# Tile addresses at one residue modulo 512 bytes, and the transposed input loaded into another tile, in a two-layer hybrid encoder trunk

## The chip, the cores and the metric

One core of one Trainium2 chip runs the whole program in one launch. The metric is the device time of one execution in microseconds (us); a kernel's time is the median of its runs. An execution that the hardware profiler records has a time of its own, and beside it a span, from the first instruction to the last.

## The reference, cut to what matters

Two layers over 256 tokens of width 2048. In each layer the normalised input `h` is multiplied by one wide matrix, `w_in`, and four branches (a recurrence, a differential attention, a latent attention and an attention into 256 memory tokens) are computed from parts of the product, gated, projected by `w_branch`, merged and projected by `w_out`:

```python
for l in range(DEPTH):                       # 2 layers
    h = _rms_norm(x, norm_g[l])              # x: (1, 256, 2048), float32
    p = h @ w_in[l]                          # (2048, 14784)
    ...
    mem_n = _rms_norm(mem, mem_norm_g[l])    # mem: (1, 256, 2048)
    y_d = _mem_attention(m_q, mem_n, mem_w_kv[l], mem_qk_g[l])
    gates = gate_in.reshape(B, S, N_BRANCH, BRANCH_WIDTH)
    merges = merge_in.reshape(B, S, N_BRANCH, D_MODEL)
    z = None
    for bi, y in enumerate((y_a, y_b, y_c, y_d)):
        zb = jax.nn.sigmoid(merges[:, :, bi]) * (
            (y.astype(x.dtype) * jax.nn.silu(gates[:, :, bi])) @ w_branch[l, bi])
        z = zb if z is None else z + zb
    x = x + z @ w_out[l]
```

All of it is float32. The kernel writes each large product as three products of rounded halves: `hi*hi + hi*lo + lo*hi`.

## The kernel before, in words

**The weight stream.** `jobs` (L491) lists the large products of a layer in the order in which TensorE is to run them: the keys and values of the memory (`mem_w_kv`, two jobs of 512 columns), the recurrence's columns of `w_in` (`e_u`, four jobs), then the other columns of `w_in`, `w_branch` and `w_out`. `main` (L564) walks that list. For every two blocks of 128 weight rows it loads a tile `raww` from HBM by a DMA on SP's queue (L584, three buffers); for each block, `split` (L166) rounds the weights to a tile `whi` on ScalarE (ACT) and puts the rest into `wlo` on VectorE (DVE), five buffers each. `product` (L624) issues three matmuls per block and output bank. In most jobs the activations are the stationary operand, 128 columns at a time (512 bytes in each partition), and `whi` or `wlo` is streamed, 512 columns wide (2,048 bytes). In the jobs with `tpos` set (the recurrence's columns and the gates) it is the other way round: slices of `whi` and `wlo` are stationary and the activations are streamed, 256 columns wide.

**The activations.** `mT`, the transposed memory, lies in the tiles S0 to S7. `hT`, the normalised input transposed, lies in T1h (the rounded half) and T1l (the rest), 16 blocks each. The gated branch results lie in ygh and ygl. The merged branches, `z`, are transposed by `z_prep` (L797) for the `w_out` jobs, two blocks at a time, into eight different places: X, iA, BK with qr, q1, T1h, k1, T1l, V1.

**Where tiles lie.** The pool `work` gives each tag its place in the order in which the tags are first asked for, in steps of 32 bytes. In the built program the starts of the tiles, in bytes modulo 512 (the residue), are:

| tiles | residue before | residue after |
|---|---|---|
| raww, whi, wlo, q1, Z | 448 | 128 |
| T1h, T1l, V1, raw | 416 | 128 |
| PT, X, S0 to S7, U, ygh | 320 | 128 |
| E, jk | 480 | 128 |
| iA, BK, qr, k1, ygl, sg, yT, r1 to r3 | 224 | 128 |

Every slice that a matmul takes of these tiles as an operand of 512 bytes or more starts a multiple of 512 bytes into its tile, so the residue of the tile is the residue of the operand.

**The start of the program.** `mem_prep(0)` (L349) loads the transposed memory into U and ygh by eight DMAs on ACT's queue and splits it into S0 to S7, while the two `mem_w_kv` jobs run. `x_first` (L406) then prepares `hT` of the first layer. It loads the transposed input (`xT`, four DMAs of 512 KB, L414) into the same places, three quarters into U and one into ygh, once the memory's blocks there are used up. Squares on ACT (L420), sums on DVE (L423 to L427), a matmul with ones (L430), a power on POOL (L433), a copy, two transposes on TensorE (L438) and a copy (L440) give the tile r4, the inverse norms spread over the partitions. Then eight chunks of two blocks are multiplied by gain and norm on DVE (L449) and split: ACT writes T1h, DVE writes T1l (L451). The event `("hT", 0)` (L454) is set after the eighth chunk, and the first `w_in` job waits for it (L525). Afterwards `token_sums` (L386) loads the memory once more, not transposed, into Z, for the norms of the memory.

**What sets the order.** The Python program runs generators (lanes) beside `main`; a scheduler then orders the instructions of each engine by a simulated timeline. `high_priority` lifts instructions in that order, and `issue_after` keeps one behind another. The weights' loads, splits and evacuations run with the priority HP. `self.last` holds the last split's two instructions, so that `issue_after(self.last[1])` puts an instruction behind the newest `wlo`. A job may have a `kready`, an event that each of its 128-row blocks waits for; before, the first memory job and the `w_out` jobs have one.

Of the kernel before, what the change touches and what calls it, by code (L numbers as in the profile page):

```python
# [29 lines left out]
C_ID, C_MF, C_MB, C_BLK, C_CEN, C_B2, C_MH, C_IF, C_OH, C_N = (  # L30
    0, 128, 256, 384, 512, 640, 642, 658, 690, 694)
# [14 lines left out]
XE = 5.0  # L46
# [7 lines left out]
def _constants():  # L54
    c = np.zeros((128, C_N), np.float32)
    c[:, C_ID:C_ID + 128] = np.eye(128)
    s = np.arange(128)[:, None] % 64
    t = np.arange(64)[None, :]
    c[:, C_MF:C_MF + 64] = s < t
    c[:, C_MF + 64:C_MF + 128] = s <= t  # L60
    c[:, C_MB:C_MB + 64] = s > t
    c[:, C_MB + 64:C_MB + 128] = s >= t
    blk = (np.arange(128)[:, None] // 64 == np.arange(128)[None, :] // 64).astype(np.float32)
    c[:, C_BLK:C_BLK + 128] = blk
    c[:, C_CEN:C_CEN + 128] = np.eye(128) - blk / 64
    c[:, C_B2:C_B2 + 2] = blk[:, [0, 64]]
    c[:, C_MH:C_MH + 16] = -0.5
# [45 lines left out]
class Builder:  # L113
# [65 lines left out]
        self.nc.gpsimd.tensor_tensor(ss, ss, self.cst[:, C_MH:C_MH + n], op=ALU.pow)  # L179

    def small(self, n):
        return self.t("small", [128, 16], bufs=6)[:, :n]


    def setup(self):
        nc, a = self.nc, self.a
# [162 lines left out]
    def mem_prep(self, l):  # L349

        nc, a = self.nc, self.a
        T = [self.t(f"S{i}", [128, 4, 256], F32R) for i in range(8)]
        X3 = self.t("U", [128, 3, 4, 256])
# [18 lines left out]
        for i in range(8):  # L372
            if not l and 1 <= i <= 4:
                with self.tc.issue_after(self.last[0]):
                    load(i + 3)
            if not l and i == 3:
                with self.tc.issue_after(self.fetch):
                    nc.sync.dma_start(self.cst, a["consts"])
            for kk in (2 * i, 2 * i + 1):
                j, k = kk // 4, kk % 4  # L380
                with self.tc.high_priority(2 * HP if kk < (4 if l else 2) else 0):
                    self.split(T[j][:, k], T[4 + j][:, k], X[j][:, k], scale=g[:, kk:kk + 1])
                self.ev.add(("mT", l, kk))
            yield 0.0

    def token_sums(self, src, rs):  # L386
# [16 lines left out]
        self.rsqrt(rs, 2, 1.0 / D, EPS)  # L403
        yield

    def x_first(self):  # L406

        nc, a = self.nc, self.a
        yield from self.until(("mT", 0, 15))
        X3 = self.t("U", [128, 3, 4, 256])  # L410
        X = [X3[:, j] for j in range(3)] + [self.t("ygh", [128, 4, 256])]
        for j in range(4):
            with self.tc.issue_after(self.last[0]):
                nc.scalar.dma_start(X[j], a["xT"][:, 4 * j:4 * j + 4])  # L414

        sq = self.t("T1l", [128, 4, 1024])
        yield XE
        for j in range(4):
            with self.tc.issue_after(self.last[0]):
                nc.scalar.activation(sq[:, j], X[j].rearrange("p k t -> p (k t)"), AF.Square)  # L420
            if j % 2:
                with self.tc.issue_after(self.last[1]):
                    nc.vector.tensor_tensor(sq[:, j - 1], sq[:, j - 1], sq[:, j], op=ALU.add)  # L423
            yield
        nc.vector.tensor_tensor(sq[:, 0], sq[:, 0], sq[:, 2], op=ALU.add)
        nc.vector.tensor_tensor(sq[:, 0, 0:512], sq[:, 0, 0:512], sq[:, 0, 512:1024], op=ALU.add)
        nc.vector.tensor_tensor(sq[:, 0, 0:256], sq[:, 0, 0:256], sq[:, 0, 256:512], op=ALU.add)  # L427
        ps = self.pa()
        for tt in range(2):
            self.mm(ps[:, 2 * tt:2 * tt + 2], sq[:, 0, tt * 128:tt * 128 + 128], self.ones)  # L430
        rs = self.small(2)
        nc.vector.tensor_scalar(rs, ps[:, 0:4:2], 1.0 / D, EPS, op0=ALU.mult, op1=ALU.add)
        nc.gpsimd.tensor_tensor(rs, rs, self.cst[:, C_MH:C_MH + 2], op=ALU.pow)  # L433
        ex = self.t("sq", [128, 2, 128])
        nc.vector.tensor_copy(ex, rs[:, :, None].to_broadcast([128, 2, 128]))
        ps = self.pa()[:, :256]
        for tt in range(2):
            self.tr(ps[:, tt * 128:tt * 128 + 128], ex[:, tt])  # L438
        rb = self.t("r4", [128, 256], bufs=1)
        self.copy(rb, ps)  # L440
        yield
        g = self.v["gains", 0][:, 16:32]
        hi = self.t("T1h", [128, 16, 256], F32R)
        lo = self.t("T1l", [128, 16, 256], F32R)
        for j in range(8):
            xs = X[j // 2][:, j % 2 * 2:j % 2 * 2 + 2]
            for k in range(2):
                with self.tc.issue_after(self.last[1]):
                    nc.vector.scalar_tensor_tensor(xs[:, k], xs[:, k], g[:, 2 * j + k:2 * j + k + 1], rb,  # L449
                                                   op0=ALU.mult, op1=ALU.mult)  # L450
            self.split(hi[:, 2 * j:2 * j + 2], lo[:, 2 * j:2 * j + 2], xs)  # L451
            yield
        self.v["hT", 0] = (hi, lo)
# [37 lines left out]
    def jobs(self, l):  # L491
        a = self.a
# [26 lines left out]
        out = []  # L519
# [621 lines left out]
    def rw_prep(self, l, ft, U, pos):  # L1141
# [7 lines left out]
        def col(p):  # L1149
            return cols[:, p:p + 1]  # L1150

        b2 = cst[:, C_B2:C_B2 + 2]
# [194 lines left out]
    def rw_finish(self, l, ft, U, unit):  # L1347
# [2 lines left out]
        cols = self.v["cols", l]  # L1350
        v = U[:, 8 + ft]
        kds, sq, yg = unit[4], *unit[-2:]
        b2 = cst[:, C_B2:C_B2 + 2]

        def col(p):
            return cols[:, p:p + 1]
# [271 lines left out]
```

## Time and profile before

| | us |
|---|---|
| median of 3 runs | 2039.71 |
| lowest and highest run | 2037.15, 2041.34 |
| the profiled execution | 2037.85 |
| its span | 2036.1 |
| PE busy in the span | 2012.8 |
| DVE busy | 1433.0 |
| ACT busy | 1114.3 |

PE is TensorE's matmul stream, PEld its loading of stationary operands, which overlaps with the matmuls. Matmuls are pipelined, so the durations of neighbours overlap, and the pace of a stretch is read from the starts of its rows and not from their durations. The granted clock is TensorE's, as a share of the full one; it is 0.995 in the mean of the span. In names of the trace the number of a tile is left out: `q` is q1, `k` is k1, `V` is V1, `S` is any of S0 to S7, `r` any of r1 to r4. L95 is a helper through which all calls of DVE and ACT go, L156 one through which all matmuls go, L161 the transposes.

### The profile page before, as it was taken

What the parts mean: (1) busy time and instruction counts of PE and PEld (TensorE: products, weight loads), DVE (VectorE), ACT (ScalarE), POOL (GpSimd) and SP (SyncE); (2) the same over time, 40 slices, a digit from 0 to 9 for tenths busy, and PEclk for the clock granted to TensorE, in tenths of its full rate; (3) what the DMA queues carried; (4) which work ended last, traced back from release to release, by engine and by line L of the source; (5) the groups of instructions that cost most, each with busy time, mean ns of one, the idle gap of its engine ahead of it and who ended that gap; (6) DMA issues with size and microseconds to landing.
All of it is one profiled execution on the core that took longest, in us unless ns stands there. A gap on an engine that the chain in (4) does not pass through costs nothing.

```text
span 2036.1 us, 33810 instructions
## 1 busy us (share of the span) xinstructions
PE 2012.8 (99%) x12054; PEld 1688.6 (83%) x12054; DVE 1433.0 (70%) x3134; ACT 1114.3 (55%) x2293; POOL 147.9 (7%) x178
## 2 busy tenths in 40 slices
PE   9899999999999999999999999999999999999999
PEld 7798997778877877888889989987788878788887
DVE  6888898877787865648565658775577777565564
ACT  6756576455455544555465565755555554454443
POOL 1101112001100000100000000110011100000000
PEclk9899999999999999999999999999999999999999
DMA  8555655545565655765766656564556555456565
GB/s 275 181 177 160 196 179 179 171 136 159 166 203 168 181 164 158 222 189 191 243 191 181 186 151 192 166 194 140 151 172 187 173 169 180 150 168 200 185 197 187
DMA packets 222313, 367.34 MB, mean 180 GB/s; under 512 B 40576, under 2 KB 60800, under 8 KB 221824
## 3 DMA queue, kind: packets, MB, share of 16 engines
q1 hardware_dynamic: 218752, 356.31, 57.6%
q10 hardware_dynamic: 3168, 8.39, 1.1%
q8 instruction: 94, 1.54, 0.3%
q0 software_dynamic: 224, 0.49, 0.2%
q14 instruction: 75, 0.61, 0.1%
HBM read 357.78 MB, written 11.53 MB: 181 GB/s over the span
## 4 chain that ended last, share of the span: by engine, by line
PE 92%; DMA 3%; DVE 3%; issue 1%; ACT 1%; SPq 0%; POOL 0%; DVEq 0%; ACTq 0%; POOLq 0%
PE mm L156 82%; PE pr L156 5%; PE pa L156 2%; PE pa L161 2%; DVE wlo L95 1%; DMA raww<-in_w_in 1%; DMA raww<-in_mem_w_kv 1%; PE pr L161 0%; ACT whi L95 0%; DMA TT<-yd 0%; DVE half L95 0%; DVE BK L95 0%; DVE U L95 0%; DMA sc<-S 0%; DVE sq L95 0%
## 5 line engine op out<-in xcount | busy, mean ns | idle before, releaser
L95 DVE TENSOR_TENSOR wlo<-raww,whi 128x512 fp32r<-128x512 f32 (+2 forms) x1300 | 863.9, 674 | 468.8 <-ACT whi L95 463.8
L95 ACT ACTIVATE whi<-raww 128x512 fp32r<-128x512 f32 (+2 forms) x1300 | 789.7, 617 | 731.1 <-PE mm L156 538.0
L156 PE MATMUL mm<-whi,T1l 128*128 128x512 f32 (+2 forms) x1472 | 573.4, 392 | 0.0
L156 PE MATMUL mm<-wlo,T1h 128*128 128x512 f32 (+2 forms) x1440 | 569.6, 396 | 1.3 <-DVE wlo L95 1.1
L156 PE MATMUL mm<-whi,T1h 128*128 128x512 f32 (+2 forms) x1472 | 533.3, 394 | 1.6 <-ACT whi L95 1.6
L156 PEld LDWEIGHTS mm<-whi,T1h 128*128 128x128 f32 x1472 | 274.9, 188 | 62.8 <-ACT whi L95 2.3
L156 PEld LDWEIGHTS mm<-whi,T1l 128*128 128x128 f32 x1472 | 276.4, 188 | 58.6 <-issue 0.7
L156 PEld LDWEIGHTS mm<-wlo,T1h 128*128 128x128 f32 x1440 | 270.2, 188 | 62.5 <-DVE wlo L95 3.9
L156 PE MATMUL mm<-T1l,whi 128*128 128x256 f32 x960 | 271.9, 284 | 4.7 <-DVE T1l L95 4.7
L156 PE MATMUL mm<-T1h,whi 128*128 128x256 f32 x960 | 271.6, 284 | 2.3 <-ACT T1h L95 2.3
L156 PE MATMUL mm<-T1h,wlo 128*128 128x256 f32 x960 | 272.2, 285 | 0.4 <-DVE wlo L95 0.4
L156 PEld LDWEIGHTS mm<-T1l,whi 128*128 128x128 f32 x960 | 182.4, 190 | 5.6 <-DVE T1l L95 5.0
L156 PEld LDWEIGHTS mm<-T1h,whi 128*128 128x128 f32 x960 | 182.3, 190 | 3.1 <-ACT T1h L95 2.5
L156 PEld LDWEIGHTS mm<-T1h,wlo 128*128 128x128 f32 x960 | 182.0, 190 | 1.0 <-DVE wlo L95 0.8
L156 PE MATMUL mm<-wlo,ygh 128*128 128x512 f32 (+1 forms) x296 | 117.0, 397 | 0.0
L156 PE MATMUL mm<-whi,ygl 128*128 128x512 f32 (+1 forms) x296 | 115.7, 392 | 0.0
L156 PE MATMUL mm<-whi,ygh 128*128 128x512 f32 (+1 forms) x296 | 112.7, 400 | 0.0
L156 PE MATMUL mm<-whi,S 128*128 128x512 f32 x256 | 84.9, 408 | 2.6 <-ACT whi L95 2.1
L179 POOL TENSOR_TENSOR small<-small,cst 128x4 f32<-128x4 f32 (+3 forms) x45 | 52.0, 1157 | 395.1 <-DVE small L95 375.7
L156 PEld LDWEIGHTS mm<-whi,ygh 128*128 128x128 f32 x296 | 55.4, 188 | 12.3 <-issue 0.7
L156 PEld LDWEIGHTS mm<-whi,ygl 128*128 128x128 f32 x296 | 55.7, 188 | 11.9 <-issue 0.3
L156 PEld LDWEIGHTS mm<-wlo,ygh 128*128 128x128 f32 x296 | 55.7, 188 | 11.2 <-issue 0.7
(319 smaller groups left out, 2173.0 us busy)
## 6 DMA issues: line engine op xcount, KB each, us to landing
raww<-in_w_in SPq DMA_DIRECT2D x432, 512.0 KB, 3.6
raww<-in_w_branch SPq DMA_DIRECT2D x64, 512.0 KB, 4.3
raww<-in_w_out SPq DMA_DIRECT2D x64, 512.0 KB, 4.5
raww<-in_mem_w_kv SPq DMA_DIRECT2D x29, 512.0 KB, 4.2
raww<-in_w_in SPq DMA_DIRECT2D x16, 384.0 KB, 3.3
raww<-in_w_in SPq DMA_DIRECT2D x16, 320.0 KB, 3.6
raww<-in_w_in SPq DMA_DIRECT2D x16, 256.0 KB, 2.7
Z<-in_mem ACTq DMA_DIRECT2D x2, 1024.0 KB
```

What stands on the lines that cost most here:

```text
L95: return g(out, *args, **kw)
L156: return self.nc.tensor.matmul(out, lhsT=lhsT, rhs=rhs, start=start, stop=stop).ins
L161: self.nc.tensor.transpose(out, in_, self.ident[:k, :k])
L179: self.nc.gpsimd.tensor_tensor(ss, ss, self.cst[:, C_MH:C_MH + n], op=ALU.pow)
```

## The change

Three edits:

1. **Addresses.** The constants' tile is 10 columns shorter (a table of two columns is read out of a larger one with a stride, and the column of exponents has 8 entries and not 16). The tiles gains, cols, mrs, xss and bm, whose sizes are no multiples of 512 bytes, and small (now with 5 buffers and not 6), are asked for first, in `setup`. All tiles after them start at residue 128. No operation is added or removed by it.
2. **Another tile for the transposed input.** `xT` goes into Z, which nothing else uses at that time, as a whole. Its four DMAs are issued in `mem_prep`, with its chunks 3 to 6. Z is then used by `token_sums` after the last split of the input.
3. **The norms' chain.** The instructions from the squares to r4 are issued without waiting for the weights' splits, and with the priority 2 HP. The sums go into one accumulator. The chunks of the input are each held behind the split of the chunk two before, and each sets an event of its own, `("hT", 0, j)`; the first `w_in` job waits for the first chunk only, and each of its blocks for its own chunk.

The core of the diff:

```diff
+        for tag, n, dt in (("gains", 32, F32), ("cols", P_N + 29, F32), ("mrs", 2, F32), ("xss", 8, F32),
+                           ("bm", 256, U8)):
+            self.t(tag, [128, n], dt)
+        self.small(2)
...
+            if not l and i >= 3 and i < 7:
+                self.x_load(i - 3)
...
+    def x_load(self, j):
+        if j == 0:
+            self.v["xT"] = self.t("Z", [128, 16, 256])
+        with self.tc.issue_after(self.last[0]):
+            self.nc.scalar.dma_start(self.v["xT"][:, 4 * j:4 * j + 4], self.a["xT"][:, 4 * j:4 * j + 4])
...
-        X3 = self.t("U", [128, 3, 4, 256])
-        X = [X3[:, j] for j in range(3)] + [self.t("ygh", [128, 4, 256])]
...
+            with soon(2 * HP):
+                nc.scalar.activation(sq[:, j], X[:, 4 * j:4 * j + 4].rearrange("p k t -> p (k t)"), AF.Square)
+                if j:
+                    nc.vector.tensor_tensor(sq[:, 0], sq[:, 0], sq[:, j], op=ALU.add)
...
-                with self.tc.issue_after(self.last[1]):
+                with self.tc.issue_after(done[j - 2] if j > 1 else self.last[1]):
                     nc.vector.scalar_tensor_tensor(xs[:, k], xs[:, k], g[:, 2 * j + k:2 * j + k + 1], rb,
                                                    op0=ALU.mult, op1=ALU.mult)
-            self.split(hi[:, 2 * j:2 * j + 2], lo[:, 2 * j:2 * j + 2], xs)
+            done.append(self.split(hi[:, 2 * j:2 * j + 2], lo[:, 2 * j:2 * j + 2], xs)[1])
+            self.ev.add(("hT", 0, j))
...
-            out.append(Job(w_in, KT, O_U + i, n, True, hT, self.e_u(l, i // 128), ("hT", l)))
+            out.append(Job(w_in, KT, O_U + i, n, True, hT, self.e_u(l, i // 128), ("hT", l, 0) if l + i == 0 else
+                           ("hT", l), (lambda k: ("hT", 0, min(k // 2, 7))) if l + i == 0 else None))
```

Two places show how the built program moves. On ACT, at the first layer's normalised input: `r` is the tile with the norms, T1h the rounded input, V the values of the memory, evacuated at the end of the second memory job. Before:

```order
L95 ACTIVATE whi_590<-raww_581 128x512
L393 DMA Z_631<-in_mem 128x2048 x2
L95 ACTIVATE V_126_597<-mm_394 128x512
L95 ACTIVATE V_126_597<-mm_407 128x512
L95 ACTIVATE whi_656<-raww_654 128x512
L95 ACTIVATE r_103_503<-pa_500 128x256
L95 ACTIVATE T1h_539<-U_304 128x512 x6
L95 ACTIVATE T1h_539<-ygh_305 128x512 x2
```

After:

```order
L94 ACTIVATE r_92_436<-pa_433 128x256
L94 ACTIVATE E_712<-E_712 128x64
L94 ACTIVATE whi_562<-raww_550 128x512
L94 ACTIVATE T1h_460<-Z_243 128x512
L94 ACTIVATE whi_578<-raww_576 128x512
L94 ACTIVATE T1h_460<-Z_243 128x512
L94 ACTIVATE whi_588<-raww_576 128x512
L94 ACTIVATE T1h_460<-Z_243 128x512
L94 ACTIVATE whi_604<-raww_602 128x512
L94 ACTIVATE whi_611<-raww_602 128x512
L94 ACTIVATE T1h_460<-Z_243 128x512
L94 ACTIVATE V_131_618<-mm_405 128x512
```

The norms' tile and the first four chunks of T1h stood behind the evacuation of V and stand ahead of it now, one chunk for each one or two weight blocks.

On PE, at the end of the second memory job (banks mm_394 and mm_407 before, mm_405 and mm_416 after) and the start of the first `w_in` job. Before:

```order
L156 MATMUL mm_407<-wlo_546,S_8_106 128x512
L156 MATMUL mm_407<-whi_545,S_12_110 128x512
L156 MATMUL pa_492<-ones,T1l_310 128x2 x2
L161 MATMUL pa_500<-cst,sq_498 128x128 x2
L156 MATMUL mm_660<-T1h_539,whi_557 128x256
L156 MATMUL mm_686<-T1h_539,whi_557 128x256
L156 MATMUL mm_660<-T1l_540,whi_557 128x256
```

After:

```order
L155 MATMUL mm_416<-whi_562,S_14_112 128x512
L155 MATMUL mm_637<-T1h_460,whi_578 128x256
L155 MATMUL mm_654<-T1h_460,whi_578 128x256
L155 MATMUL mm_405<-wlo_563,S_14_112 128x512
L155 MATMUL mm_405<-whi_562,S_18_116 128x512
L155 MATMUL mm_416<-wlo_563,S_14_112 128x512
L155 MATMUL mm_416<-whi_562,S_18_116 128x512
L155 MATMUL mm_637<-T1l_461,whi_578 128x256
```

The matmul with ones and the two transposes stood between the last memory matmul and the first of the `w_in` job; now they stand 32 or more matmuls earlier, within the memory job. In the first layer after that some of the small matmuls of the branches stand some tens of large matmuls later or earlier than before (mostly up to 60, a few more than 100); in the second layer the order of PE's matmuls is the same as before.

More of the change, by code (lines that the diff above doesn't have):

```diff
@@ L27 @@
 O_U, O_DQ, O_DK, O_DV, O_LAT, O_MQ, O_G, O_M = 0, 1792, 2304, 2816, 3328, 4032, 4544, 6592
-C_ID, C_MF, C_MB, C_BLK, C_CEN, C_B2, C_MH, C_IF, C_OH, C_N = (
-    0, 128, 256, 384, 512, 640, 642, 658, 690, 694)
+C_ID, C_MF, C_MB, C_BLK, C_CEN, C_MH, C_IF, C_OH, C_N = (
+    0, 128, 256, 384, 512, 640, 648, 680, 684)
 P_SH, P_W0, P_A0, P_KK, P_KA, P_RK, P_GG, P_GB = 0, 42, 50, 58, 62, 66, 70, 74
@@ L65, in _constants @@
     c[:, C_CEN:C_CEN + 128] = np.eye(128) - blk / 64
-    c[:, C_B2:C_B2 + 2] = blk[:, [0, 64]]
-    c[:, C_MH:C_MH + 16] = -0.5
+    c[:, C_MH:C_MH + 8] = -0.5
     c[:, C_IF:C_IF + 32] = (10000.0 ** (-np.arange(0, 64, 2) / 64.0))[None, :]
@@ L181, in small @@
     def small(self, n):
-        return self.t("small", [128, 16], bufs=6)[:, :n]
+        return self.t("small", [128, 16], bufs=5)[:, :n]
     def setup(self):
@@ L409, in x_first @@
         yield from self.until(("mT", 0, 15))
-        X3 = self.t("U", [128, 3, 4, 256])
-        X = [X3[:, j] for j in range(3)] + [self.t("ygh", [128, 4, 256])]
+        X = self.v["xT"]
+        sq = self.t("T1l", [128, 4, 1024])
+        soon = self.tc.high_priority
         for j in range(4):
[L413 to L421, printed above, removed]
-                with self.tc.issue_after(self.last[1]):
-                    nc.vector.tensor_tensor(sq[:, j - 1], sq[:, j - 1], sq[:, j], op=ALU.add)
-            yield
@@ L425, in x_first @@
[L425 to L440, printed above, removed]
+            with soon(2 * HP):
+                nc.scalar.activation(sq[:, j], X[:, 4 * j:4 * j + 4].rearrange("p k t -> p (k t)"), AF.Square)
+                if j:
+                    nc.vector.tensor_tensor(sq[:, 0], sq[:, 0], sq[:, j], op=ALU.add)
@@ new lines, in x_first @@
+            yield
+        with soon(2 * HP):
+            nc.vector.tensor_tensor(sq[:, 0, 0:512], sq[:, 0, 0:512], sq[:, 0, 512:1024], op=ALU.add)
+            nc.vector.tensor_tensor(sq[:, 0, 0:256], sq[:, 0, 0:256], sq[:, 0, 256:512], op=ALU.add)
+            ps = self.pa()
+            for tt in range(2):
+                self.mm(ps[:, 2 * tt:2 * tt + 2], sq[:, 0, tt * 128:tt * 128 + 128], self.ones)
+            rs = self.small(2)
+            nc.vector.tensor_scalar(rs, ps[:, 0:4:2], 1.0 / D, EPS, op0=ALU.mult, op1=ALU.add)
+            nc.gpsimd.tensor_tensor(rs, rs, self.cst[:, C_MH:C_MH + 2], op=ALU.pow)
+            ex = self.t("sq", [128, 2, 128])
+            nc.vector.tensor_copy(ex, rs[:, :, None].to_broadcast([128, 2, 128]))
+            ps = self.pa()[:, :256]
+            for tt in range(2):
+                self.tr(ps[:, tt * 128:tt * 128 + 128], ex[:, tt])
+            rb = self.t("r4", [128, 256], bufs=1)
+            self.copy(rb, ps)
@@ L444, in x_first @@
         lo = self.t("T1l", [128, 16, 256], F32R)
+        done = []
+        self.v["hT", 0] = (hi, lo)
         for j in range(8):
-            xs = X[j // 2][:, j % 2 * 2:j % 2 * 2 + 2]
+            xs = X[:, 2 * j:2 * j + 2]
             for k in range(2):
-                with self.tc.issue_after(self.last[1]):
+                with self.tc.issue_after(done[j - 2] if j > 1 else self.last[1]):
                     nc.vector.scalar_tensor_tensor(xs[:, k], xs[:, k], g[:, 2 * j + k:2 * j + k + 1], rb,
                                                    op0=ALU.mult, op1=ALU.mult)
-            self.split(hi[:, 2 * j:2 * j + 2], lo[:, 2 * j:2 * j + 2], xs)
+            done.append(self.split(hi[:, 2 * j:2 * j + 2], lo[:, 2 * j:2 * j + 2], xs)[1])
+            self.ev.add(("hT", 0, j))
             yield
-        self.v["hT", 0] = (hi, lo)
         self.ev.add(("hT", 0))
@@ L1150, in col @@
             return cols[:, p:p + 1]
-        b2 = cst[:, C_B2:C_B2 + 2]
+        b2 = cst[:, C_BLK:C_BLK + 128:64]
         wup = self.t("wup", [128, 2, 128], bufs=1)
@@ L1352, in rw_finish @@
         kds, sq, yg = unit[4], *unit[-2:]
-        b2 = cst[:, C_B2:C_B2 + 2]
+        b2 = cst[:, C_BLK:C_BLK + 128:64]
         def col(p):
```

## The prediction

> **What bounds the kernel now.** I read the chain of work that ended last, then the costliest groups, then the longest pieces of that chain in order of time, then PE's timeline. The chain by engine:
>
> ```profile
> PE 92%; DMA 3%; DVE 3%; issue 1%; ACT 1%; SPq 0%; POOL 0%; DVEq 0%; ACTq 0%; POOLq 0%
> ```
>
> So TensorE's matmuls are the bound nearly throughout, and a faster ACT, DVE or DMA would be worth little. The groups that make it up:
>
> ```profile
> L156 PE MATMUL mm<-whi,T1l 128*128 128x512 f32 (+2 forms) x1472 | 573.4, 392 | 0.0
> L156 PE MATMUL mm<-wlo,T1h 128*128 128x512 f32 (+2 forms) x1440 | 569.6, 396 | 1.3 <-DVE wlo L95 1.1
> L156 PE MATMUL mm<-whi,T1h 128*128 128x512 f32 (+2 forms) x1472 | 533.3, 394 | 1.6 <-ACT whi L95 1.6
> L156 PE MATMUL mm<-T1l,whi 128*128 128x256 f32 x960 | 271.9, 284 | 4.7 <-DVE T1l L95 4.7
> L156 PE MATMUL mm<-T1h,whi 128*128 128x256 f32 x960 | 271.6, 284 | 2.3 <-ACT T1h L95 2.3
> L156 PE MATMUL mm<-T1h,wlo 128*128 128x256 f32 x960 | 272.2, 285 | 0.4 <-DVE wlo L95 0.4
> L156 PE MATMUL mm<-wlo,ygh 128*128 128x512 f32 (+1 forms) x296 | 117.0, 397 | 0.0
> L156 PE MATMUL mm<-whi,S 128*128 128x512 f32 x256 | 84.9, 408 | 2.6 <-ACT whi L95 2.1
> ```
>
> There is next to no idle time before them, but their mean durations overlap and are no pace. The pace stands in two long pieces of the chain (start, length, count), the first of 512-wide matmuls, the second of 256-wide ones:
>
> ```profile
> 818.65 106.75 PE mm L156 x457
> ...
> 1095.01 53.49 PE mm L156 x452
> ```
>
> 106.75 / 457 is 233.6 ns for each 512-wide matmul, and 53.49 / 452 is 118.3 ns for each 256-wide one. Two things can then shorten the program: a faster pace, and the few places where PE stands still. The largest of those, after the first DMA has come in, is the start of the first `w_in` job:
>
> ```profile
> 56.90 0.39 PE L156 MATMUL mm<-whi,S 128*128 128x512 f32 x1
> 57.12 0.50 PE L156 MATMUL pa<-ones,T1l 128*128 128x2 f32 x4
> 59.12 0.41 PE L161 MATMUL pa<-cst,sq 128*128 128x128 f32 x2 [1.49 <-issue]
> 61.82 0.79 PE L156 MATMUL mm<-T1h,whi 128*128 128x256 f32 x2 [2.30 <-ACT T1h L95]
> 67.31 0.58 PE L156 MATMUL mm<-T1l,whi 128*128 128x256 f32 x1 [4.69 <-DVE T1l L95]
> 67.69 0.41 PE L156 MATMUL mm<-T1h,wlo 128*128 128x256 f32 x1
> 67.90 0.41 PE L156 MATMUL mm<-T1h,whi 128*128 128x256 f32 x1
> ...
> 71.10 0.35 PE L156 MATMUL mm<-T1l,whi 128*128 128x256 f32 x1
> ...
> 72.00 0.28 PE L156 MATMUL mm<-T1h,wlo 128*128 128x256 f32 x1
> ```
>
> The memory job's last matmul starts at 56.90. The norms' chain follows it, and steady work comes only with the first T1l at 67.31. The granted clock (in the rows below the third figure from the end, ahead of the DMA share and GB/s) is low in that gap and for 4 us after it:
>
> ```profile
> 57.00:67.30 10.30, 1.83 (x10) 1.20 (x8) 10.03 (x31) 7.01 (x12) 0.72 (x1) 0.69 0.71 274
> 67.30:72.00 4.70, 4.69 (x24) 4.69 (x25) 4.70 (x10) 0.75 (x3) 0.00 (x0) 0.58 0.04 7
> ```
>
> **The norms' chain (edits 2 and 3).** What stands in the gap is the tile with the norms, then sixteen products on DVE, then the splits:
>
> ```profile
> 59.56 0.38 ACT L95 ACTIVATE r<-pa 128x256 f32<-128x256 f32 x1 [0.93 <-PE pa L161]
> ...
> 60.23 4.83 DVE L95 SCALAR_TENSOR_TENSOR U<-U,gains,r 128x256 f32<-128x256 f32 x12
> ...
> 66.57 0.69 DVE L95 TENSOR_TENSOR T1l<-U,T1h 128x512 fp32r<-128x512 f32 x1
> ...
> 67.30 3.10 DVE L95 TENSOR_TENSOR T1l<-U,T1h 128x512 fp32r<-128x512 f32 x5
> ```
>
> DVE does all the products before the first T1l, and the first job waits for it. The change puts the chain under the second memory job, and each block of the first job waits only for its own chunk. Removed: from the end of the last memory matmul (56.90 + 0.23 = 57.13) to 67.31, 10.2 us, less 0.7 us of small matmuls that remain, 9.5. The slow clock after it goes too: from 67.69 to 67.90 a 256-wide matmul takes 0.21 and later 0.118, 18 of them until 71.10, 1.7 us. Together 11.2.
>
> What is late next is DVE in the first job. Per chunk it has two products (4.83 / 12 x 2 = 0.80), a T1l (3.10 / 5 = 0.62) and two `wlo`, which I take at the same 0.62 each since tile and operation are alike: 2.7 us. PE needs 2 blocks x 12 matmuls x 0.118 = 2.8 us for it. The cover is thin, but in the new order the first chunks are finished under the memory job. Bounds: nothing lost, or all of the gap if DVE falls behind. I take 0.7 us. **The term is -10.5 us.**
>
> The loads of `xT` move a little ahead on ACT's queue, by a step or two of `mem_prep`: with Z free from the start they no longer wait for U. Queued behind the issuing instruction are only ACT's next splits, 0.3 to 0.5 us per issue, and that was so before. What they collide with is the weights of the first memory job. The only stall there now, and how full the DMA engines are:
>
> ```profile
> 33.73 0.39 PE L156 MATMUL mm<-whi,S 128*128 128x512 f32 x1
> 35.62 0.74 PE L156 MATMUL mm<-whi,S 128*128 128x512 f32 x2 [1.50 <-ACT whi L95]
> ...
> 30.00:40.00 10.00, 8.50 (x30) 6.23 (x29) 2.68 (x5) 5.98 (x10) 0.00 (x0) 0.86 0.78 292
> ```
>
> It costs 35.62 - 33.73 - 0.23 = 1.7 us, and 1.4 more by the clock (0.86 over 10 us). The bytes are the same before and after, so I carry it over as it is. Bounds: it goes (3 us gained), or all 2.1 MB at 292 GB/s stand ahead of the weights (7.2 us, 4 more than now).
>
> **The addresses (edit 1).** No instruction changes; the question is whether a matmul runs faster when its two operands start at the same residue. The trace has one natural trial. In `w_out`, twelve matmuls at a time use each of eight tiles as stationary operand, with the same streamed tiles (residue 448), the same bank order and the same neighbours. Only q1 lies at 448 as well:
>
> ```profile
> 958.91 0.63 PE L156 MATMUL mm<-whi,V 128*128 128x512 f32 x2
> ...
> 961.71 0.64 PE L156 MATMUL mm<-whi,X 128*128 128x512 f32 x2
> ...
> 964.50 0.63 PE L156 MATMUL mm<-whi,iA 128*128 128x512 f32 x2
> ...
> 967.30 0.63 PE L156 MATMUL mm<-whi,BK 128*128 128x512 f32 x2
> ...
> 970.10 0.62 PE L156 MATMUL mm<-whi,q 128*128 128x512 f32 x2
> ...
> 972.85 0.63 PE L156 MATMUL mm<-whi,T1h 128*128 128x512 f32 x2
> ...
> 975.65 0.62 PE L156 MATMUL mm<-whi,k 128*128 128x512 f32 x2
> ```
>
> The starts of the tiles give V1 (416) 2.80 us for twelve, X (320) 2.79, iA (224) 2.80, BK with qr (224) 2.80, T1h (416) 2.80, and q1 (448) 2.75. That is 229 ns a matmul against 233, 4.0 ns less. It isn't a property of 448 alone: in the 256-wide jobs the stationary `whi` lies at 448 too, under a stream at 416, and 118.3 ns for 256 columns is no better than 233.6 for 512. So I take the difference of the residues as what counts, and the change makes every difference zero.
>
> Of 512-wide matmuls with unequal residues there are 1472 + 1440 + 1472 in the T1 rows, 3 x 296 with ygh and ygl, 256 + 128 with S and 480 with six other tiles of `w_out`: 6,136, some narrower, 6,000 in full widths. 6,000 x 4.0 = 24.0 us. For the 2,880 256-wide ones no row has equal residues; bounds 0 and the same share, 118.3 x 4.0 / 233 = 2.0 ns. I take 2.0, since their pace per column now equals that of the 512-wide ones: 5.8 us. As PE is 92% of the chain I count 0.92 x 29.8: **-27.4 us.** Where PE gets ahead, DMA is next (3% of the chain), but the loads have room.
>
> Against this stands a rule of the Trainium skill, "SBUF — State Buffer", section "Who interferes with whom": TensorE has two independent read ports, one for the stream and one for loading weights, and waits on nobody. By that rule the addresses would give nothing and the sum would be the first term alone; the q1 rows disagree by 4 ns.
>
> **The sum.** 2037.85 (profiled execution) - 10.5 - 27.4 = 1999.9. The median of the runs is 1.9 above that execution, so 2002 against 2039.71.
>
> **The rivals.**
> - *Addresses do nothing* (the page's rule as a mechanism): q1's lead would come from something else in its place, for instance what ACT and DVE do at that time. For: only 96 matmuls carry the term. Against: twelve-matmul stretches before and after it are alike to 0.01 us. 2039.7 - 10.5 = 2029.
> - *The gap stays*: DVE falls behind in the first job, and what the chain gained is given back there. For: 2.7 of 2.8 us per chunk. Against: the first T1h matmuls now stand among the memory job's. 2039.7 - 27.4 = 2012.
> - *Equal starts collide* (the slower side): two streams in step could hit the same part of the memory at each moment, and the pace falls. For: single paces do vary with the address; X alternates, with 0.24 between these two starts:
>
> ```profile
> 938.11 0.40 PE L156 MATMUL mm<-wlo,X 128*128 128x512 f32 x1
> 938.35 0.63 PE L156 MATMUL mm<-whi,X 128*128 128x512 f32 x2
> ```
>
>   Against: q1 is the only equal case, and is faster. It decides as soon as a 512-wide matmul loses 10.5 us / (6,000 + 1,440) = 1.4 ns. At the mirror of my term, +27.4 us, the time is 2057.
> - *More than I count*: over all equal neighbours the gain could exceed q1's, whose stretch borders on others. At 6 ns and 3 ns it is 36 + 9 us; with the gap and the early stall (11.2 + 3) 59 us, 1980.
>
> **How the numbers follow.** My forecast, both terms, 0.62; addresses nothing 0.18; the gap stays 0.08; collision 0.07; more than I count 0.05. The range 1986 to 2032 takes in the forecast with its unknown costs (half of the extra gain below; above, addresses nothing with 3 us lost to the earlier loads) and leaves out the collision and the largest gain. A measurement of this kernel can tell about 0.2%, 4 us, from no change. Faster by more than that: 0.62 + 0.08 + 0.05 and 0.15 of the 0.18, 0.90. Within it: the remaining 0.03, where the gap's gain is eaten too. Slower: 0.07.
>
> **What would show it.** Long pieces of the chain at 229 ns (512-wide) and 116 (256-wide); 233 and 118 mean the addresses do nothing, more means a collision. The second layer has PE's matmuls in the same order, so its length alone tells the second term. At 57 us the timeline should show `mm<-T1h` right behind the last `mm<-whi,S` and a granted clock of 1.00; a wait on T1l there is DVE falling behind. A longer wait for `raww` ahead of 36 us would be the earlier loads. I am wrong if the pace is unchanged, or if the gap reappears later in the first job.

## The result and the profile after

The changed kernel takes 2007.84 us (median of 4 runs, 2006.46 to 2008.54), the one before 2038.82 beside it (2037.15 to 2041.34). The ratio is 0.9846, 95% interval [0.9829, 0.9863]: 31 us less. The forecast was 2002 with a range of 1986 to 2032. The sum forecast 37.9 us less; where the other 7 went, and why the two terms came out as they did, takes the rest of this text.

**The start of the first `w_in` job.** PE's timeline where 10.2 us of gap stood before (start, length, engine, line, operation, shapes; in brackets the wait and what ended it):

```profile
55.55 0.62 PE L155 MATMUL mm<-whi,S 128*128 128x512 f32 x2
56.00 0.40 PE L155 MATMUL mm<-T1h,whi 128*128 128x256 f32 x2
...
56.93 0.40 PE L155 MATMUL mm<-whi,S 128*128 128x512 f32 x1
57.16 0.40 PE L155 MATMUL mm<-T1l,whi 128*128 128x256 f32 x2
57.40 0.28 PE L155 MATMUL mm<-T1h,wlo 128*128 128x256 f32 x1
57.52 0.28 PE L155 MATMUL mm<-T1h,whi 128*128 128x256 f32 x1
...
60.76 0.39 PE L155 MATMUL mm<-T1h,wlo 128*128 128x256 f32 x1 [0.33 <-DVE wlo L94]
```

The first T1h matmuls stand among the memory job's last ones, and from 57.16 on the starts lie 0.12 apart. DVE is late once, by 0.33 us. The gap is gone, as the first term had it.

**A new gap.** Some 26 us later PE stands still where it did not before:

```profile
83.28 0.28 PE L155 MATMUL mm<-T1h,wlo 128*128 128x256 f32 x1
86.98 0.39 PE L155 MATMUL mm<-T1h,whi 128*128 128x256 f32 x1 [3.42 <-ACT whi L94]
```

The clock pays for it once more. The stretch behind it (from and to, length, then the busy time of PE, PEld, DVE, ACT and POOL, each with its number of instructions in brackets; the last figures are the granted clock, DMA's share and GB/s):

```profile
87.40:91.20 3.80, 3.52 (x18) 3.32 (x17) 3.80 (x7) 3.80 (x8) 0.00 (x0) 0.58 0.28 73
```

At a clock of 0.58, 18 matmuls take 3.80 us; at 0.120 each they would take 2.2. That is 1.6 us lost, and with the 3.6 us of gap over 5 us in all.

**The pace.** Two long stretches of the second layer, the first of 512-wide matmuls, the second of 256-wide ones (columns as above). Before:

```profile
1815.00:1915.00 100.00, 100.00 (x430) 80.39 (x429) 52.86 (x80) 50.00 (x84) 0.00 (x0) 1.00 0.63 193
1095.50:1145.50 50.00, 50.00 (x425) 50.00 (x425) 29.34 (x52) 25.28 (x46) 0.00 (x0) 1.00 0.57 169
```

After:

```profile
1790.00:1890.00 100.00, 100.00 (x442) 82.78 (x442) 53.85 (x82) 52.54 (x88) 0.00 (x0) 1.00 0.64 197
1075.00:1125.00 50.00, 50.00 (x419) 50.00 (x418) 29.23 (x51) 24.66 (x45) 0.00 (x0) 1.00 0.57 168
```

PE is busy all the time in all four, at full clock. 512-wide matmuls come faster (442 in 100 us for 430), 256-wide ones slower (419 in 50 us for 425). Each row lies in a longer stretch without a pause; from its first and last start the pace is 233.3 ns before and 226.9 after for 512-wide ones (505 matmuls), 118.3 and 120.0 for 256-wide ones (451 matmuls). Over all matmuls in the kernel that stand directly before another of the same width, pauses left out, the means are 233 and 227.8, 118.3 and 119.9; 384- and 320-wide ones stay within 0.5 ns, near 175 and 146.5. The forecast had 229 and 116.

**Where the time lies.** PE executes the same large matmuls in all these kernels, nearly in the same order, so the start of the n-th one can be compared between traces. How much later than in the changed kernel it is, in us (worked out from the starts; layer 0 is the first layer, layer 1 the second; the experiments' names are explained below):

| kernel | n = 190 (56 us) | 384 (80 us) | 430 (92 us) | 4572 (layer 1 begins) | last |
|---|---|---|---|---|---|
| before | 0.4 | 11.1 | 5.3 | 19.7 | 31.4 |
| e1_addresses | -0.1 | 10.8 | 5.1 | 13.3 | 12.9 |
| e2_chain | 0.8 | 0.3 | 2.9 | 14.1 | 25.8 |
| e4_later | 1.4 | 1.7 | -0.4 | 2.3 | 0.1 |
| e7_rows | 6.3 | 6.0 | 0.7 | 1.3 | 1.9 |
| e8_noload | -1.8 | -1.9 | -7.6 | -8.9 | -9.2 |
| e9_pieces | 1.4 | 1.4 | -4.3 | 4.5 | 2.9 |
| e10_before_noload | -2.5 | 8.3 | 2.5 | 17.7 | 31.2 |
| e5_weights64 | 0.8 | 0.2 | 1.3 | 0.2 | -1.4 |
| e6_pair | 1.6 | 1.2 | 2.0 | -1.6 | -11.5 |
| best | -0.2 | -1.1 | -6.7 | 6.1 | -3.4 |

The traces differ by up to 3 us already at n = 96, so differences between columns say more than a single figure. One execution of each kernel is traced, and it can lie anywhere among that kernel's runs: those of e4 and e8 are about 4 us below their medians, those of e9 and best 2 and 5 above. The row of before reads: 10.7 us gained up to 80 us (the gap), 5.8 of them given back at the new gap, 14.4 more gained in the rest of layer 0, 11.7 in layer 1.

### The profile page after: what moved, and what is told of

Its sections match the earlier page's. It is cut to its first block, busy times and chain, and to the rows that moved or that the text cites. A ratio compares the mean times of both kernels' runs of the same rounds, so it can differ in the third digit from the quotient of the medians.

```text
span 2004.7 us, 33815 instructions
## 1 busy us (share of the span) xinstructions
PE 1986.8 (99%) x12054; PEld 1691.3 (84%) x12054; DVE 1432.0 (71%) x3134; ACT 1112.9 (56%) x2293; POOL 149.3 (7%) x178
## 5 line engine op out<-in xcount | busy, mean ns | idle before, releaser
L155 PE MATMUL mm<-whi,T1l 128*128 128x512 f32 (+2 forms) x1472 | 567.2, 388 | 0.0
L155 PE MATMUL mm<-wlo,T1h 128*128 128x512 f32 (+2 forms) x1440 | 562.5, 391 | 0.0
L155 PEld LDWEIGHTS mm<-whi,ygl 128*128 128x128 f32 x296 | 55.6, 188 | 10.5
L155 PEld LDWEIGHTS mm<-wlo,ygh 128*128 128x128 f32 x296 | 55.7, 188 | 10.2 <-issue 0.3
```

The costliest lines, as they stand in the source:

```text
L155: return self.nc.tensor.matmul(out, lhsT=lhsT, rhs=rhs, start=start, stop=stop).ins
```

## The experiments

The theory: the two terms are real and act apart; the address term is a property of the two operands' start addresses; and the 6 us given back come from the memory's second load, which the change moves from 56 to 73 us.

**e1_addresses and e2_chain: each part alone.** e1 is the kernel before with edit 1; e2 is the changed kernel without it. (Edit 1 as it stands in the change.)

```diff
...
-        return self.t("small", [128, 16], bufs=6)[:, :n]
+        return self.t("small", [128, 16], bufs=5)[:, :n]
...
+        for tag, n, dt in (("gains", 32, F32), ("cols", P_N + 29, F32), ("mrs", 2, F32), ("xss", 8, F32),
+                           ("bm", 256, U8)):
+            self.t(tag, [128, n], dt)
+        self.small(2)
...
```

> The kernel before with the first edit alone (addresses). If the residues carry the pace, whatever stands at the start: 512-wide matmuls at 228 ns (before 233), 256-wide at 120 ns (before 118), so about 5,900 x -5.1 ns + 2,880 x +1.6 ns = -25.5 us, near 2013 us, and the gap from 57 to 67 us stays as it was. Rival, the gain beyond the first 200 us comes from the other order of the instructions in the first layer: near 2030 us or above, with the pace at 233 ns.

> The changed kernel without the first edit (tiles at several residues as before). If the two parts add up: the chain alone is worth 11 us at the start of the first w_in job and loses 5 to 6 of them again near 83 us, where ACT stands before the memory's second load into Z: -5 to -6 us, near 2033 us, pace 233 and 118 ns. Rival, the loss near 83 us comes from the addresses (256-wide matmuls, DVE or the splits slower at one residue): no wait there, -11 us, near 2028 us.

Measured: e1 2018.78 us (2017.9 to 2019.44), ratio 0.9898 [0.9883, 0.9913], 20.8 us less than before; e2 2032.24 us (2030.92 to 2034.67), ratio 0.9968 [0.9955, 0.998], 7.3 less in the runs. e1's two stretches of the second layer:

```profile
1800.00:1900.00 100.00, 100.00 (x442) 82.79 (x442) 54.09 (x82) 51.36 (x86) 0.00 (x0) 1.00 0.64 197
1088.00:1138.00 50.00, 50.00 (x419) 50.00 (x418) 29.52 (x51) 24.92 (x44) 0.00 (x0) 1.00 0.56 166
```

The counts are those of the whole change: addresses alone set the pace. In layer 1 e1 gains all that the change gains there (12.1 us to its 11.7 by the table), in layer 0 only 6.4 us. From the start of the large matmul n = 1800 to that of n = 2200 (337 to 456 us) it takes 4.4 us longer than the kernel before, where the pace alone would make it 2.1 us shorter. There PE waits for `whi` at 352 us, and near 404 us a pause between small matmuls is longer than before; behind it the clock is slow (0.77, where before has 1.00 over the same time):

```profile
352.50 0.73 PE L155 MATMUL mm<-whi,T1h 128*128 128x512 f32 x2 [1.24 <-ACT whi L94]
...
405.00:420.00 15.00, 14.34 (x149) 11.32 (x150) 9.64 (x21) 8.29 (x22) 0.00 (x0) 0.77 0.36 107
```

e2 has the gap's 10.8 us at n = 384 and loses 8.4 of them, against before, by n = 430 with the old pace (232.9 and 118.3 ns in the mean): what is given back near 83 us has nothing to do with addresses. The two parts alone make 28.1 us together, the whole 31. On top of the chain the addresses bring 24.4 us (2032.24 - 2007.84).

**pace: matmuls alone.** One streamed tile and sixteen stationary tiles whose starts lie 0, 32, 64, ... 480 bytes behind the stream's; no other engine works.

> The matmuls alone, 48 of a kind in a row, no other engine at work: the stream starts at residue 128, sixteen stationary tiles (a to p) start 0, 32, ... 480 bytes further on; widths 512, 384 and 256; then both operands at the same residue, at sixteen places. This leaves out the whole computation. If the difference of the residues sets the pace: 512-wide near 227 ns at a difference of 0 and 232 to 234 at 96 to 480, 256-wide near 120 at 0 and 117 at 480 or 32 (whichever way it counts), and no dependence on the place where both are equal. Rival, the place itself counts (128 is good for 512-wide, whatever the other operand): the pace varies over the sixteen equal places as much as over the differences. Second rival, what counts is how the operands lie to what ACT and DVE do: no dependence at all here, one pace for each width.

Measured, from the last 43 distances between starts of each stretch, ns a matmul by the distance (stationary less stream):

| distance, bytes | 0 | 32 | 64 | 96 | 128 | 160 | 192 | 224 |
|---|---|---|---|---|---|---|---|---|
| 512 wide | 226.7 | 233.2 | 233.3 | 234.3 | 233.4 | 233.4 | 228.9 | 233.3 |
| 256 wide | 119.9 | 118.3 | 113.3 | 118.7 | 118.6 | 120.1 | 117.8 | 117.8 |
| 384 wide | 173.6 | 173.5 | 173.3 | 173.3 | 176.1 | 176.7 | 173.3 | 176.7 |

(For 512 wide at 0, the stretch at 256 is given; the one at 0 begins with starts 427 ns apart.) Distances of 256 to 480 repeat the row to 0.1 ns: the period is 256 bytes and not 512. With both operands at the same residue, sixteen different places give 226.7 to 227.3 and 120.0. So it is the distance that counts, neither the place nor what ACT and DVE do at the time. That disposes of the rival "addresses do nothing", and explains the table of the kernel: before, the 256-wide matmuls stood at 448 - 416 = 32 bytes, 118.3 ns here as there; at 0 they take 119.9, here as there.

**e5_weights64: the same distance law in the kernel.** All weight tiles lie 64 bytes further.

```diff
+                if not nxt[0]:
+                    self.t("pad0", [128, 16])
                 hi = self.t("whi", [128, 512], F32R, bufs=self.LOOK)
                 lo = self.t("wlo", [128, 512], F32R, bufs=self.LOOK)
+                if not nxt[0]:
+                    self.t("pad1", [128, 48])
```

> The kernel after the change, with the weight tiles whi and wlo 64 bytes further and all larger tiles behind them 256 bytes further: a weight now starts 64 bytes behind the activation's residue, modulo 256. Theory (the pace goes by the distance from the stream's start to the stationary operand's, modulo 256 bytes, as in the run of matmuls alone): 256-wide matmuls, whose stationary operand is the weight, stand at 64 and take 113.3 ns for 119.9, 2,880 x 6.6 = 19 us less; 512-wide ones, whose stream is the weight, stand at -64 = 192 and take 228.9 ns for 227.8 or less, some 5,900 x 1 to 2 = 6 to 13 us more; in all 6 to 13 us less than after, 1995 to 2002 us. Rival 1 (any two residues that differ are slow): 512-wide back at 233 ns, 256-wide at 118, 2030 us. Rival 2 (the run of matmuls alone does not carry over to the kernel): paces and time as after, 2008 us.

Measured: 2005.33 us (2004.4 to 2006.64), ratio 0.9831 [0.9817, 0.9845]. The two stretches of the second layer:

```profile
1785.00:1885.00 100.00, 100.00 (x439) 82.05 (x438) 53.34 (x81) 51.08 (x85) 0.00 (x0) 1.00 0.64 197
1075.00:1125.00 50.00, 50.00 (x444) 50.00 (x443) 31.29 (x58) 27.11 (x50) 0.00 (x0) 1.00 0.57 170
```

Both go the way that the distances foretell: 512-wide a little slower (439 for 442), 256-wide faster (444 for 419). Rivals 1 and 2 are out. The means over the kernel are 229.3 and 115.0 ns; 115.0 is not 113.3, and so the time is 3 us above the range expected. Some stretches of 256-wide matmuls keep 113 to 114 ns from end to end, others 117 to 118.

**e6_pair: the better distance for each width.** whi and wlo become two parts of one tile, whose place in it depends on the job; the last lines of the diff put a small temporary tile into the place of r4.

```diff
-                hi = self.t("whi", [128, 512], F32R, bufs=self.LOOK)
-                lo = self.t("wlo", [128, 512], F32R, bufs=self.LOOK)
+                pair = self.t("whi", [128, 1088], F32R, bufs=self.LOOK)
+                o = (16, 528) if j.tpos else (0, 576)
+                hi, lo = (pair[:, q:q + 512] for q in o)
...
-        tmp = self.t("small2", [128, 4, 64], bufs=1)[:, :n]
+        tmp = self.t("r4", [128, 256], bufs=1).rearrange("p (h d) -> p h d", h=4)[:, :n]
```

> The kernel after the change, with whi and wlo as two parts of one tile: at distance 0 from the activations' residue where the weight is the stream (512, 384 and 320 wide), at distance 64 where it is the stationary operand (256 wide). Theory (distance modulo 256 bytes): 512-wide stay at 227.8 ns, 256-wide go from 119.9 to 113.3 ns: 2,880 x 6.6 = 19 us less than after, of which nine tenths arrive, 1989 to 1992 us. Rival: the tile comes free only when both parts have been read, and the splits come later: paces as in the theory, but more gaps of PE beside ACT's and DVE's splits, 1995 to 2008 us.

Measured: 1996.28 us (1995.02 to 1996.94), ratio 0.9785 [0.9771, 0.9799], 11.6 us below the changed kernel and the fastest of this study. Its stretches:

```profile
1775.00:1875.00 100.00, 100.00 (x443) 82.81 (x442) 54.39 (x82) 51.22 (x86) 0.00 (x0) 1.00 0.65 199
1073.00:1123.00 50.00, 50.00 (x443) 50.00 (x442) 31.36 (x57) 26.86 (x51) 0.00 (x0) 1.00 0.57 169
1660.00:1675.00 15.00, 15.00 (x130) 15.00 (x129) 9.92 (x27) 7.87 (x15) 1.04 (x2) 1.00 0.69 192
```

512-wide matmuls keep their pace and 256-wide ones become faster, but the third row, of 256-wide ones too, shows another rhythm: 130 in 15 us, 117 to 118 ns, where 113 would make 134. The mean is 115.7 ns, 4.2 less than after. Times 2,880 that is 12.1 us, and 11.5 are measured at the last matmul. The distances hold; the 113.3 ns expected for every 256-wide matmul does not.

**pace2: why 113 here and 118 there.** Matmuls alone again, 256 wide, at finer distances, six stretches at each.

```diff
+SHIFT = (0, 16, 32, 40, 48, 52, 56, 60, 64, 68, 72, 76, 80, 96, 128, 192)
+LEAD = (0, 64, 96, 128, 192, 320)
...
+        for n in LEAD:
+            if n:
+                nc.tensor.matmul(banks[0][:, :n], lhsT=sta[i][:, o:o + 128], rhs=mov[:, 0:n], start=True, stop=True)
```

> 256-wide matmuls alone, no other engine at work (leaves the whole computation out): stationary tiles at 0 to 192 bytes from the stream's start in finer steps, and at each distance six stretches of 48 matmuls, each but the first behind one matmul of another width (64 to 320). Tells why the 256-wide ones of the kernel with two-part weight tiles took 113 ns in some stretches and 118 in others. Theory (two rhythms, set by how a stretch starts): at distance 64, stretches of 113 and of 118 ns here too, the same from the first matmuls of a stretch to its last. Rival (ACT, DVE or DMA at work beside them): 113 ns at distance 64 in all six stretches. Either way distance 0 gives 120 ns in all of them.

Two stretches at 64 bytes, one at 52 and one at 76 (here the columns are PE, PEld, ACT, POOL, clock, DMA and GB/s):

```profile
288.50:293.50 5.00, 5.00 (x44) 5.00 (x44) 0.00 (x0) 0.00 (x0) 1.00 0.01 3
294.20:299.20 5.00, 5.00 (x46) 5.00 (x45) 0.00 (x0) 0.00 (x0) 1.00 0.00 0
...
191.20:196.20 5.00, 5.00 (x47) 5.00 (x46) 0.00 (x0) 0.00 (x0) 1.00 0.00 0
391.80:396.80 5.00, 5.00 (x47) 5.00 (x46) 0.00 (x0) 0.00 (x0) 1.00 0.00 0
```

The first two have the same operands and differ only in the one matmul ahead of them: 117.8 and 113.4 ns from the starts. Of the six stretches at 64 bytes three take 113.4 and three 117.7 to 117.8: two rhythms with no other engine at work, so the rival is out. Which of the two a stretch takes goes with the matmul ahead of it, but each start was run once, so that it decides is not shown. At 52 and at 76 bytes all six take 113.3; at 56, 60, 68 and 72 none does (117.6 to 119.8). Whether 52 or 76 would hold 113 in the kernel was not tried.

**e4_later: the order on ACT.** Now the new gap. ACT's timeline before it, in the changed kernel:

```profile
73.41 1.75 ACTq L399 DMA_DIRECT2D Z<-in_mem  x2
73.92 0.62 ACT L94 ACTIVATE whi<-raww 128x512 fp32r<-128x512 f32 x1
76.76 1.15 ACT L94 ACTIVATE whi<-raww 128x512 fp32r<-128x512 f32 x2 [2.23 <-DMA raww<-in_w_in]
80.08 1.06 ACT L94 ACTIVATE Z<-Z 128x1024 f32<-128x1024 f32 x1 [2.16 <-DMA Z<-in_mem]
...
83.50 1.06 ACT L94 ACTIVATE Z<-Z 128x1024 f32<-128x1024 f32 x1 [0.51 <-DMA Z<-in_mem]
...
86.31 2.18 ACT L94 ACTIVATE whi<-raww 128x512 fp32r<-128x512 f32 x4
```

The memory's second load is issued at 73.41 us, when Z is free of x. ACT then waits 2.16 us for it to square Z, and the next weight splits (86.31), which PE waits for, stand behind those squares. The first idea was that this order is the fault; e4 lets the squares come later.

```diff
-        yield XE
+        yield 14.0
```

> The changed kernel with one number changed: token_sums waits 14 us of the planner's time instead of 5 before its squares, so that on ACT they stand behind the evacuation of the first job and two more weight splits, one by one between pairs of splits. If the wait of 3.7 us near 83 us (and the slow clock behind it) is ACT standing before the load into Z, it goes: 4 to 5.5 us less than the changed kernel, near 2003 us. Rival, the weights themselves were late there (DMA), or DVE: the wait stays, near 2008 us.

Measured: 2010.3 us (2006.57 to 2012.3), ratio 0.9856 [0.9841, 0.9871]: no gain. By the table 2.1 us are gained between n = 384 and 430 and lost again by the end of layer 0. The squares do stand behind the splits now, and the splits are late all the same. e4's ACT:

```profile
74.99 1.34 ACTq L399 DMA_DIRECT2D Z<-in_mem  x2
...
78.28 1.15 ACT L94 ACTIVATE whi<-raww 128x512 fp32r<-128x512 f32 x2 [2.15 <-DMA raww<-in_w_in]
...
86.26 1.15 ACT L94 ACTIVATE whi<-raww 128x512 fp32r<-128x512 f32 x2 [1.59 <-DMA raww<-in_w_in]
```

The weights themselves have not landed. So the order on ACT is not the whole cause, and the load came under suspicion.

**e8_noload and e10_before_noload: the load left out, after and before.**

```diff
-        X = self.t("Z", [128, 2, 2048])
+        X = self.v["xT"].rearrange("p (t k) d -> p t (k d)", t=2)
         ss = self.t("xss", [128, 2, 4])
-        for tt in range(2):
-            with self.tc.issue_after(self.last[0]):
-                nc.scalar.dma_start(X[:, tt], src[tt * 128:tt * 128 + 128])
```

(e10 does the same in the kernel before, with the squares taken of U and ygh.)

> The kernel after the change; leaves out the second load of the memory's rows in layer 0 (the squares are taken of what stands in Z, so the memory's norms are of other numbers). Tells ACT's share from the load's. Theory (both have a share: the squares stand ahead of the weights' splits, and the load slows the weights): the gaps of 1.5 to 3 us with DMA ahead of the splits go, 74 to 80 us, and of the one at 83 us some 2 us stay if the squares still stand ahead of the splits; 2003 to 2005 us. Rival 1 (the order on ACT alone): the gap at 83 us of 3.7 us stays or moves with the squares, 2008 us. Rival 2 (the load alone): no gap over 1 us from 70 to 90 us, 2002 us.

> The kernel before the change; leaves out the second load of the memory's rows in layer 0 (the squares are taken of the normed input, so the memory's norms are of other numbers). Theory (before, the load ran while PE stood idle for other reasons from 57 to 67 us, and cost nothing; the change took that cover away): the gap stays 9 to 11 us and the time within 2 us of before, 2036 to 2039 us. Rival (the 2 MB cost 6 to 8 us in whichever order, as they do after the change): 2031 to 2033 us.

Measured: e8 2001.74 us (1997.4 to 2002.76), ratio 0.9812 [0.9798, 0.9826]; e10 2038.59 us (2035.51 to 2041.4), ratio 0.9993 [0.9985, 1.0002]. The stretch from 72 to 84 us, in the changed kernel:

```profile
72.00:84.00 12.00, 11.56 (x97) 11.35 (x95) 6.50 (x15) 5.72 (x11) 0.00 (x0) 1.00 0.95 340
```

and in e8:

```profile
72.00:84.00 12.00, 12.00 (x102) 12.00 (x101) 8.08 (x17) 10.88 (x28) 0.70 (x1) 1.00 0.62 185
```

With the load the DMA engines are full (0.95, 340 GB/s); without it the weights need 185 GB/s and PE has no gap over 0.1 us there, though ACT's squares still stand among the splits. By the table 5.7 us come between n = 384 and 430 (from -1.9 to -7.6). So the load is the cause and ACT's order only where it showed (e8's rival 2). Before, the same load costs nothing: left out, it moves the time by 0.07%, and the interval takes in 1; the gap stays (10.8 us between n = 190 and 384). The row of that gap in the kernel before shows why,

```profile
56.20:67.30 11.10, 2.63 (x13) 1.86 (x11) 10.21 (x31) 7.60 (x13) 0.72 (x1) 0.72 0.73 277
```

and ACT's queue issued the load at its start:

```profile
56.16 0.82 ACTq L393 DMA_DIRECT2D Z<-in_mem  x2
```

PE was idle and DMA ran at 277 GB/s: the gap was the cover of the load.

**e7_rows: the load earlier.** It goes into U and ygh, and is issued behind x's squares.

```diff
+    def mem_rows(self, src):
+        X3 = self.t("U", [128, 3, 1024])
+        X = [X3[:, j] for j in range(3)] + [self.t("ygh", [128, 1024])]
+        for j in range(4):
+            with self.tc.issue_after(self.last[0]):
+                self.nc.scalar.dma_start(X[j], src[j // 2 * 128:j // 2 * 128 + 128, j % 2 * 1024:j % 2 * 1024 + 1024])
+        return X
...
+        rows = self.mem_rows(a["mem"][0])
...
```

> The kernel after the change, with the rows of the memory for layer 0's norms loaded into the tiles U and ygh right behind x's squares (about 50 us) and no more into Z (73 us). Theory (6 us are lost near 83 us since this load must wait for Z): PE's gaps of 74 to 87 us are gone, since neither ACT's squares nor the load stand beside the weights of that stretch; the difference at the matmul of 75 us stays at -11 us up to layer 0's middle, 2002 to 2004 us. Rival (2 MB cost the weights' loads as much wherever they lie): gaps of 4 to 6 us now at 57 to 75 us, 2008 us.

Measured: 2008.94 us (2007.04 to 2009.73), ratio 0.9847 [0.9833, 0.9861]: as after. The load was issued still earlier than meant, at 35 us, and the same 6 us are now lost there, in the memory job:

```profile
36.00:47.00 11.00, 9.85 (x46) 7.75 (x44) 8.62 (x27) 2.97 (x7) 0.72 (x1) 1.00 0.98 356
```

and on ACT:

```profile
35.26 0.34 ACTq L397 DMA_DIRECT2D U<-in_mem  x1
...
45.72 1.15 ACT L94 ACTIVATE whi<-raww 128x512 fp32r<-128x512 f32 x2 [6.00 <-DMA raww<-in_mem_w_kv]
```

DMA is full (0.98) and ACT waits 6.00 us for weights. The gap at 83 us is gone (the table's 6.0 at n = 384 becomes 0.7 at 430). The rival was right in the cost: in one block the 2 MB cost 6 us here as they did at 73 us, both times beside the weights' loads.

**e9_pieces: the load in eight pieces**, the first two together, the others 6 to 8 us apart.

```diff
-        for tt in range(2):
-            with self.tc.issue_after(self.last[0]):
-                nc.scalar.dma_start(X[:, tt], src[tt * 128:tt * 128 + 128])
-        yield XE
+        for i in range(8):
+            with self.tc.issue_after(self.last[0]):
+                s = slice(i % 4 * 512, i % 4 * 512 + 512)
+                nc.scalar.dma_start(X[:, i // 4, s], src[i // 4 * 128:i // 4 * 128 + 128, s])
+            yield 6.0
```

> The kernel after the change, with the second load of the memory's rows in eight pieces of 256 KB, each issued some two to four weight splits (3 to 6 us) behind the one before, where two of 1 MB stood one behind the other. Theory (the 2 MB lay on DMA engines that were full from 72 to 84 us, 370 to 440 GB/s, and took from the weights' share): no second of that stretch is full any more, no gap of PE over 1 us from 70 to 110 us, and most of the 5.7 us that leaving the load out brought there comes: 2002 to 2004 us. Rival 1 (any 2 MB cost the weights 6 us, wherever and however they come): small gaps in place of one, 2007 to 2008 us. Rival 2 (what costs is that ACT takes the squares ahead of splits): the squares now come later, among other splits, and cost as much there, 2006 to 2008 us.

Measured: 2007.11 us (2003.03 to 2009.51), ratio 0.9837 [0.9823, 0.9852]: no difference that can be told. The stretch:

```profile
72.00:84.00 12.00, 12.00 (x103) 12.00 (x102) 7.59 (x15) 5.13 (x10) 0.00 (x0) 1.00 0.86 263
```

Here the theory holds: DMA at 263 GB/s, PE without a gap, 5.7 us gained between n = 384 and 430 (from 1.4 to -4.3). But the kernel gives them back, 5.4 of them between n = 800 and 1160 (137 to 211 us). The memory's norms now come some 55 us later (first used on ACT at 143.93 us, in the changed kernel at 88.39), the order of the work behind them is another, and new waits stand from 140 us on, the longest of that stretch at 205 us:

```profile
205.54 0.31 PE L155 MATMUL mm<-whi,T1l 128*128 128x320 f32 x1
207.90 0.56 PE L155 MATMUL mm<-whi,T1h 128*128 128x320 f32 x2 [2.05 <-ACT whi L94]
```

The first layer ends 4.5 us later than after. Which of the moved instructions does it was not separated.

**best: e6 and e9 together.**

> Both together: whi and wlo as two parts of one tile with the distances 0 and 64, and the rows of the memory in eight pieces. Theory (the two have nothing to do with each other): 1996.3 less what the pieces bring alone, 5 us, 1990 to 1992 us. Rival (the shorter matmuls ask for weights faster, so that the pieces get in their way): 1993 to 1996 us.

Measured: 1998.53 us (1994.78 to 2003.22), ratio 0.9794 [0.9781, 0.9808]. Neither theory nor rival: the pieces bring nothing here as they brought nothing alone, and its runs scatter more. In its trace, against e6's, 6.4 us are gained between n = 384 and 430 and 11.8 are lost near 710 us, where PE waits for DVE between small matmuls and the clock falls:

```profile
708.79 0.26 PE L155 MATMUL pr<-sq,k 32*32 32x32 f32 x1 [2.62 <-DVE sq L94]
...
705.00:715.00 10.00, 7.38 (x78) 5.22 (x78) 8.77 (x18) 3.21 (x6) 0.00 (x0) 0.67 0.43 119
```

e6_pair stays the fastest.

## Why the prediction was right, and where it was not

The missing 7 us, from the medians: the chain's edits bring 7.3 us alone and not 10.5 (3.2 short); the addresses bring 24.4 on top of them and not 27.4 (3.0 short); 0.8 is the difference between the medians of before that e2 and the change were taken against.

- **The gap** (11.2 us of it removed, 0.7 lost to DVE). Right: 10.7 us by n = 384, and DVE falls behind once by 0.33 us.
- **What is late next** was looked for on DVE only. Here the step that failed is "Where PE gets ahead, DMA is next (3% of the chain), but the loads have room": the sum holds no term for the memory's second load, though the diff puts it into Z behind x. It cost nothing that can be told under the gap (e10) and 5.7 us without it (e8). What the prediction named as a way to be wrong, a gap that reappears later in the first job, is just this.
- **The loads of `xT` carried as 0.** Nearly right. The stall near 31 us waits 2.37 us in place of 1.50, but the clock stays at 1.00 over 30 to 40 us, where it was 0.86, and by n = 190 the two kernels are level (0.4 in the table):

```profile
33.95 0.73 PE L155 MATMUL mm<-whi,S 128*128 128x512 f32 x2 [2.37 <-ACT whi L94]
```

- **512-wide matmuls** (4.0 ns each from q1). Right in cause, too small: 5 ns in the mean, 6.4 in the long stretch. The twelve matmuls of q1 mixed two paces: in the trace their first six distances are 223 to 236 ns, the next five 226 to 227, and the last, to the next tile, 235.
- **256-wide matmuls** (2.0 ns faster, by the same share). Wrong in sign: 1.6 ns slower. The failed step is "their pace per column now equals that of the 512-wide ones", which took one law for both widths (per column the two even differed by 1.3% before). The bounds there, 0 to 2.0, had no loss in them.
- The two errors nearly cancel: 6,000 x 5.1 - 2,880 x 1.6 = 26 us, where the prediction had 29.8 ahead of its factor 0.92; e1 gives 20.8 alone, and 24.4 come on top of the chain. So the address term was near in size partly by luck.
- **The rule weighed there**, that TensorE loads weights and streams through independent ports and waits on nobody (the Trainium skill, "SBUF — State Buffer", section "Who interferes with whom"), would have left the pace at 233 ns. The run of matmuls alone gives 226.7 or 233.3 by nothing but the distance of two start addresses, so the trace disagrees by 6.6 ns.
- **The rivals.** "Equal starts collide" has a grain of truth: for 256-wide matmuls 0 is one of the worst distances, but it costs 1.6 ns there, and the kernel as a whole gains. "The gap stays" came true by about half its sum (5.8 of 10.7 us), by DMA and not by DVE. "More than I count" was near for the 512-wide matmuls (6 ns; 5 in the mean) and of the wrong sign for the others.

## What to carry to other kernels

Before a gap is closed, look at what runs under it: a load that costs nothing while TensorE is idle can cost nearly its whole transfer time where the DMA engines are already feeding weights (here about 6 us for 2.1 MB, which at 340 GB/s take 6.2). Judge a rescheduling by the start of the same matmul in both traces, at several places, since a gain at one place may be given back at the next. And measure an address effect with the operands alone, for each width, before one law is taken for all.

## What was not expected of the hardware

The pace of fp32r matmuls behind one another depends on the distance of the two operands' start addresses modulo 256 bytes, and differently for each width: 512 wide 226.7 ns at 0 and 228.9 at 192, but 233.2 to 234.3 at the other six multiples of 32; 256 wide 113.3 ns at its best and 119.9 at 0, 120.1 at 160. At 64 bytes the 256-wide pace has two rhythms, 113.3 and 117.8 ns, each kept for a whole stretch; at 52 and 76 bytes only the fast one was seen. The reason is open: no run shows what in the chip these distances are.
